# Retention in three bursts, its read-out turned by VectorE and DRAM, gate loads on SyncE

## The chip, the cores and the metric

The kernel runs on one core of a Trainium2 chip. The metric is the device time of one execution in microseconds (us), as the median of several runs; lower is better. Within the core TensorE (PE) multiplies matrices, VectorE (DVE), ScalarE (ACT) and GpSimd (POOL) work on tiles, and SyncE (SP) issues DMAs. ScalarE and GpSimd issue DMAs too, each in the order of its own instructions.

## The reference

Two layers of a decoder trunk on x of 512 x 1024, all float32. Each layer runs three branches of width 512 from one input projection, multiplies each by sigmoid gates after a branch projection, adds them, and goes on with an output projection and a gated MLP.

```python
for l in range(DEPTH):                       # 2 layers
    h = rmsnorm(x, norm1_g[l])
    p = h @ w_in[l]
    ...
    y_rw  = rwkv7_branch(p_rw, ...)          # branch 0
    y_ret = retention_branch(p_ret, cos, sin)  # branch 1
    y_sg  = sgu_branch(p_sg, ...)            # branch 2
    branches = jnp.stack([y_rw, y_ret, y_sg], axis=2)
    proj = jnp.einsum('bsgc,gcd->bsgd', branches, w_branch[l])
    gates = jax.nn.sigmoid(gate_logits.reshape(B, S, N_BRANCH, D_MODEL))
    x = x + jnp.sum(gates * proj, axis=2) @ w_out[l]
    x = x + conv_ffn(rmsnorm(x, norm2_g[l]), ...)
```

The retention branch, which the change rewrites, has 4 heads (q and k of 64, v of 128 columns) over 4 chunks of 128 positions; the scale and the gate at its end are applied per position and head:

```python
scores = jnp.einsum('bhnid,bhnjd->bhnij', qc, kc) * decay_in[:, None]
inner = jnp.einsum('bhnij,bhnje->bhnie', scores, vc)
kv = jnp.einsum('bhnjd,bhnje,hj->nbhde', kc, vc, k_dec)
...                                          # R_prev: running sum of kv with decay
cross = jnp.einsum('bhnid,nbhde,hi->bhnie', qc, R_prev, q_dec)
y = (inner + cross).transpose(0, 2, 3, 1, 4).reshape(B, S, RET_HEADS, RET_V_DIM)
y = y * lax.rsqrt(jnp.mean(y * y, axis=-1, keepdims=True) + EPS)
return (y.reshape(B, S, RET_V_WIDTH) * jax.nn.silu(g))
```

## The kernel before

Every large product is written as three matmuls of a high and a low part (lo x hi, hi x hi, hi x lo), each of 128 rows by 512 columns. A weight block of 128 x 512 goes through `unit`: SyncE loads it into one of three raw tiles (`wr`, line 123), ScalarE copies the high part (`sh` or `wh`, line 136), VectorE subtracts to get the low part (`sl` or `wl`, line 137), which frees the raw tile for the next load. The matmuls with both parts are line 153. `split` does the same to an activation (lines 145 and 146).

After the recurrence of branch 0, `mixer` runs through the steps of the string `SEQ` (both versions stand in the diff), in this order but for what the scheduler, which sets the order of the instructions on each engine, moves around. The steps are:

- `0`, `2` and `1`: a merge, `merge(l, br, m, ...)`: block m of the projection of branch 0, 2 or 1. It takes one weight unit, 12 matmuls into a PSUM tile `acc`, and VectorE multiplies that by the gate tile `gth` (line 1024), which comes back from DRAM (`gd`, line 1021), and adds it to the sum of the branches.
- `H`: `ret_heads` loads q and k of the retention branch, head by head, and copies parts of q (`qS`) and v (`vs`) to other partitions by DMAs on ScalarE's queue (line 882).
- `S`: one row of retention, `ret_row(read, score)`: the scores of chunk `score` (16 small matmuls), and for chunk `read` the products with scores and states (up to 32 small matmuls) into two PSUM tiles X; then ScalarE squares with a sum (`rss`, line 936), VectorE multiplies by the gate (line 938), GpSimd raises the sums to the power -1/2 (`rrr`, line 949), and ScalarE scales the four heads (line 952). `ret_states` adds 32 and 24 small matmuls (line 898) in the first two rows. There are five rows: score 0; read 0 and score 1; and so on to read 3.
- `G` and `U`: steps of branch 2 (`sgu_out`, 16 matmuls of 128 columns, line 1009; and a group of 24 matmuls of 512 columns).
- `Y`: `ret_out`: TensorE turns the 4 x 4 blocks of 128 x 128 of the scaled heads with 16 transposes (line 959) into PSUM, and `split` makes the high and low parts that the `1` merges read.

Of the kernel before, what the change touches and what calls it, by code (L numbers as in the profile page):

```python
# [17 lines left out]
S = 512  # L18
# [6 lines left out]
SEQ = "0 H 0 0 G G S U S U G S 0 G S 0 0 S 2 2 0 0 Y 2 2 1 2 1 2 1 2 1 2 1 1 1 1"  # L25
# [24 lines left out]
class Emit:  # L50
# [110 lines left out]
    def matF(self, ps, w, xs):  # L161
        for _ in self.matFg(ps, w, xs):
            pass

    def matFg(self, ps, w, xs):

        K = len(xs)
        for k0 in range(0, K, 4):
            nk = min(4, K - k0)
            hi, lo = self.unit(*w[:3], w[3] + k0 * 128, nk * 128)  # L170
            for j in range(nk):
                k = k0 + j
                sl = slice(j * 128, j * 128 + 128)
                self.mm3(ps, (hi[:, sl], lo[:, sl]), xs[k], k == 0, k == K - 1)
            yield
# [187 lines left out]
    def mixer(self, l, nst):  # L363
# [19 lines left out]
        rows = iter([(None, 0), (0, 1), (1, 2), (2, 3), (3, None)])  # L383
        for step in SEQ.split():
            if step == "S":
                self.ret_row(*next(rows))
            elif step == "G":
                ysg.append(self.sgu_out(len(ysg)))
            elif step == "H":
                self.ret_heads()  # L390
            elif step == "U":
                next(rest), next(rest)
            elif step == "Y":
                yret = self.ret_out()
            elif step == "0":
                mg.append(self.merge(l, 0, len(mg), yrw))
            elif step == "2":
                mg[m2] = self.merge(l, 2, m2, ysg, mg[m2])
                m2 += 1
            else:  # L400
                out.append(self.split(self.merge(l, 1, len(out), yret, mg[len(out)], self.nc.vector), self.f))
# [465 lines left out]
    def ret_heads(self):  # L867
# [3 lines left out]
        for j in range(4):  # L871
            t = self.r((128, 4, 128), n="qF" if j < 2 else "kF")
            self.nc.sync.dma_start(t.rearrange("p c t -> p (c t)"), self.qk[128 * j:128 * j + 128, :])
            (self.qF if j < 2 else self.kF).append(t)
# [31 lines left out]
    def ret_row(self, read, score):  # L906
# [5 lines left out]
        hd = [(j, p, h) for j in range(2) for p in range(2) for h in range(2)]  # L912
# [5 lines left out]
        if read is not None:  # L918
            v, g = self.vt[read], self.yg[read]
            for j, p, h in [(j, p, 1 - h) for j, p, h in hd]:  # L920
                i, o = 2 * j + h, h ^ j
                w = v[hv[p], 128 * i:128 * i + 128] if p == o else self.vs[read][hv[o], j, :]
                mm(o, p, X[o][hv[p], j, :], self.sc[hv[o], h, p, :], w, read == p == 0)
            for j, p, h in hd:
                if read or p:
                    o, ts = h ^ j, slice(128 * read + 64 * p, 128 * read + 64 * p + 64)
                    q = self.qS if j else self.qF[0].rearrange("p c t -> p (c t)")
                    mm(o, p, X[o][hv[p], j, :], q[hv[o], ts], self.Rs[2 * read + p][hv[o], j, :])
        if score is not None:
            for j, p, h in hd:  # L930
                ts = slice(64 * p, 64 * p + 64)
                mm(h, h ^ j, X[h][hv[h ^ j], 2, ts], self.kF[j][hv[h], score, ts], self.qF[j][hv[h], score, ts])
        if read is not None:
            sq, ss = self.u((128, 4, 128), n="rsq"), self.small((128, 4), "rss")
            for i in range(4):
                A.activation(sq[:, i, :], X[i % 2 ^ i // 2][:, i // 2, :], AF.Square, accum_out=ss[:, i:i + 1])
            for o in range(2):
                V.tensor_tensor(self.heads(g, o), X[o][:, 0:2, :], self.heads(g, o), op=MUL)
        if score is not None:
            sc = self.u((128, 2, 2, 64), n="sc")  # L940
            for h in range(2):
                V.tensor_tensor(sc[:, h], X[h][:, 2, :].rearrange("q (p t) -> q p t", t=64), self.c("le64").unsqueeze(1).to_broadcast([128, 2, 64]), op=MUL)
            self.sc = sc
            if score < 2:
                self.ret_states(4 * score, 4 + 3 * score)
        if read is not None:
            V.tensor_scalar(ss, ss, 4.0 / 128, 4e-6, op0=MUL, op1=ADD)
            rr = self.small((128, 4), "rrr")
            nc.gpsimd.tensor_tensor(rr, ss, self.c("mhalf")[:, 0:4], op=POW)
            for i in range(4):  # L950
                o = g[:, 128 * i:128 * i + 128]
                A.activation(o, o, AF.Copy, scale=rr[:, i:i + 1])

    def ret_out(self):
        out = []
        for h in range(4):
            pt = self.sm()
            for c in range(NC):
                self.tc.keep_in_program_order(self.nc.tensor.transpose(pt[:, c * 128:c * 128 + 128], self.yg[c][:, h * 128:h * 128 + 128], self.c("ident")))  # L959
            out.append(self.split(pt, self.f))  # L960
        return out
# [55 lines left out]
    def merge(self, l, br, m, y, sum=None, add=None):  # L1017

        nc = self.nc
        t = self.f(n="gth")  # L1020
        nc.gpsimd.dma_start(t, self.gd[br, m])
        ps = self.acc()
        self.matF(ps, ("wall", l, 58 + br * 4 + m // 2, m % 2 * 512), y)
# [277 lines left out]
```

## Time and profile before

| what | value |
|---|---|
| median of 3 runs | 1703.2 us (1702.57 to 1703.39) |
| profiled execution, whole | 1702.28 us |
| its span | 1700.6 us |
| granted TensorE clock, mean | 0.999 |
| busy: PE, DVE, ACT, POOL | 1692.3, 1141.6, 765.9, 245.4 us |

The span is the time between the first and the last instruction that the profiler saw in that one execution. Busy time of an engine is what its instructions took; where an engine is idle, the profile names the instruction that ended the wait. Layer 0 has its retention rows between 363 and 410 us, layer 1 between 1210 and 1255 us. In a timeline row stand start, duration, engine, line, operation, tiles, shape and count.

### The profile page before, as it was taken

Reading aid. Unit: us, or ns where it says so; the run is one execution under the profiler, and the core shown is the slowest. Engines: PE = TensorE matmul, PEld = TensorE weight load, DVE = VectorE, ACT = ScalarE, POOL = GpSimd, SP = SyncE. Lnnn points to the kernel's source line nnn. Section 1 sums busy time; section 2 is a strip of 40 time slices with the busy share of each in tenths; the row PEclk is TensorE's granted clock in tenths of the full one; section 3 lists DMA queues with packets and bytes.
Section 4 is the critical chain, followed back from the end, with each engine's and each line's share of the span. In section 5 each row is a group of like instructions: output and inputs, shape, how many; then the busy total and the mean of one; then the engine's idle time right before and its main releaser. Section 6 shows DMA issues by size and latency. Waiting matters only on the chain.

```text
span 1700.6 us, 28356 instructions
## 1 busy us (share of the span) xinstructions
PE 1692.3 (100%) x10564; PEld 1390.6 (82%) x10564; DVE 1141.6 (67%) x2032; ACT 765.9 (45%) x1341; POOL 245.4 (14%) x326
## 2 busy tenths in 40 slices
PE   9999999999999999999999999999999999999998
PEld 7888877888888888888888888778888888888887
DVE  7887856567569777653367786564765798876432
ACT  7564433535355444333255634345343554443322
POOL 1122235114100000000011203441141000000010
PEclk9999999999999999999999999999999999999999
DMA  5334566446443333243332346555364454432531
GB/s 175 91 101 151 147 151 152 141 130 194 137 149 100 96 97 99 69 119 110 115 113 80 112 142 155 148 141 161 108 210 141 132 138 123 124 107 68 155 100 55
DMA packets 151337, 214.20 MB, mean 126 GB/s; under 512 B 48416, under 2 KB 57248, under 8 KB 151200
## 3 DMA queue, kind: packets, MB, share of 16 engines
q1 hardware_dynamic: 129552, 171.62, 34.2%
q0 software_dynamic: 9600, 21.77, 4.9%
q10 hardware_dynamic: 12048, 19.00, 3.4%
q8 instruction: 83, 1.36, 0.3%
q14 instruction: 54, 0.44, 0.1%
HBM read 181.92 MB, written 23.07 MB: 121 GB/s over the span
## 4 chain that ended last, share of the span: by engine, by line
PE 99%; DMA 0%; ACT 0%; DVE 0%; issue 0%
PE acc L153 88%; PE sm L153 4%; PE sm L647 2%; PE acc L287 1%; PE sm L561 1%; PE sm L915 1%; PE acc L1009 0%; PE sm L524 0%; PE sm L523 0%; DMA g<-pcols 0%; PE sm L898 0%; PE sm L959 0%; PE sm L805 0%; PE sm L795 0%; PE sm L578 0%; PE sm L579 0%
## 5 line engine op out<-in xcount | busy, mean ns | idle before, releaser
L153 PE MATMUL acc<-lo,sh 128*128 128x512 f32 x1108 | 432.3, 390 | 0.0
L153 PE MATMUL acc<-hi,sh 128*128 128x512 f32 x1108 | 431.6, 390 | 0.0
L153 PE MATMUL acc<-hi,sl 128*128 128x512 f32 x1108 | 431.1, 389 | 0.0
L136 ACT CAST sh<-wr 128x512 fp32r<-128x512 f32 (+1 forms) x385 | 235.1, 615 | 380.2 <-PE acc L153 263.4
L137 DVE TENSOR_TENSOR sl<-wr,sh 128x512 fp32r<-128x512 f32 (+1 forms) x385 | 263.4, 687 | 170.5 <-ACT sh L136 104.8
L153 PEld LDWEIGHTS acc<-lo,sh 128*128 128x128 f32 x1108 | 208.0, 188 | 44.1 <-issue 0.7
L153 PEld LDWEIGHTS acc<-hi,sl 128*128 128x128 f32 x1108 | 208.0, 188 | 43.7 <-issue 0.3
L153 PEld LDWEIGHTS acc<-hi,sh 128*128 128x128 f32 x1108 | 208.0, 188 | 42.9 <-issue 0.2
L136 ACT CAST wh<-wr 128x512 fp32r<-128x512 f32 x194 | 120.2, 620 | 227.9 <-PE acc L153 209.2
L153 PE MATMUL acc<-lo,wh 128*128 128x512 f32 x556 | 219.4, 395 | 0.0
L153 PE MATMUL acc<-hi,wl 128*128 128x512 f32 x556 | 217.0, 390 | 0.0
L153 PE MATMUL acc<-hi,wh 128*128 128x512 f32 x556 | 216.6, 390 | 0.0
L137 DVE TENSOR_TENSOR wl<-wr,wh 128x512 fp32r<-128x512 f32 x195 | 138.9, 712 | 111.6 <-ACT wh L136 104.7
L153 PEld LDWEIGHTS acc<-hi,wl 128*128 128x128 f32 x556 | 104.4, 188 | 22.6 <-issue 0.7
L153 PEld LDWEIGHTS acc<-lo,wh 128*128 128x128 f32 x556 | 104.3, 188 | 22.6 <-issue 0.3
L153 PEld LDWEIGHTS acc<-hi,wh 128*128 128x128 f32 x556 | 104.4, 188 | 20.9
L153 PE MATMUL acc<-ah,sh 128*128 128x512 f32 x352 | 108.3, 389 | 0.0
L1077 DVE TENSOR_TENSOR fu<-acc,rsF 128x512 f32<-128x512 f32 x88 | 60.5, 689 | 62.3 <-PE acc L153 62.3
L1079 ACT ACTIVATE cv<-fu,pc 128x512 f32<-128x512 f32 x88 | 71.6, 816 | 50.4 <-DVE fu L1077 47.5
L153 PE MATMUL acc<-wl,hi 128*128 128x512 f32 x192 | 78.0, 406 | 0.0
L1080 DVE SCALAR_TENSOR_TENSOR cv<-fu,pc,cv 128x511 f32<-128x511 f32 x88 | 65.4, 746 | 18.6 <-ACT cv L1079 18.6
L153 PEld LDWEIGHTS acc<-ah,sh 128*128 128x128 f32 x352 | 66.1, 188 | 13.7
(335 smaller groups left out, 2450.1 us busy)
## 6 DMA issues: line engine op xcount, KB each, us to landing
wr<-wall SPq DMA_DIRECT2D x480, 256.0 KB, 2.7
gd<-gth ACTq DMA_DIRECT2D x48, 256.0 KB, 3.3
gth<-gd POOLq DMA_DIRECT2D x48, 256.0 KB, 3.3
wr<-wdt SPq DMA_DIRECT2D x44, 256.0 KB, 2.7
wr<-wdn SPq DMA_DIRECT2D x40, 256.0 KB, 2.7
x<-xT SPq DMA_DIRECT2D x8, 256.0 KB, 4.7
tn<-ysq POOLq DMA_DIRECT2D x32, 64.0 KB, 3.3
tab<-rot ACTq DMA_DIRECT2D x8, 256.0 KB, 3.9
```

Source lines behind the costliest of these rows:

```text
L136: self.kept((high or self.nc.scalar.copy)(hi[:, :n], raw[:, :n]))
L137: self.kept(self.nc.vector.tensor_tensor(lo[:, :n], raw[:, :n], hi[:, :n], op=SUB))
L153: i = self.nc.tensor.matmul(*x, **y, **kw)
L287: po(self.nc.tensor.matmul(pss[j], w[:, j * 128:j * 128 + 128], x, start=k == n == 0, stop=k == 7 and n == 2))
L561: i = T.matmul(pK[hv[1 - h], j, :], bk[hv[h], c, 1, :], x[hv[h], c, :], start=True, stop=True)
L647: po(T.matmul(o, l, r, start=start, stop=True, skip_group_check=True))
L915: po(T.matmul(o, lhsT, rhs, start=new[b][q], stop=stop, skip_group_check=True))
L1077: V.tensor_tensor(u, ps, self.rsF, op=MUL)
L1079: A.activation(t, u, AF.Identity, scale=self.p("cw2", j), bias=self.p("cb", j))
L1080: V.scalar_tensor_tensor(t[:, 1:], u[:, :511], self.p("cw1", j), t[:, 1:], op0=MUL, op1=ADD)
```

## The change

Retention is cut into three bursts instead of five rows: the first computes the scores of all four chunks and the first states, the second reads chunks 0 and 1 and adds the other states, the third reads chunks 2 and 3. The read-out leaves TensorE: VectorE turns 32 x 32 blocks of the scaled heads into four tiles `yz`; 16 DMAs on ScalarE's queue (64 KB each, 512 bytes a piece) write them to a DRAM tile; four SyncE loads bring it back as `yF` in the order of columns that the merges need; ScalarE and VectorE make the two parts. In `SEQ` ten merges now stand between the last `S` and the first `1`. The gate loads of the merges move from GpSimd's queue to SyncE's, in program order behind the weight's load of the same merge; those of branches 1 and 2 take their tiles from another pool. `ret_heads` loads its four tiles in another order.

```diff
@@ -22,7 +22,7 @@
 RWC, RETC, SGC = 1792, 1536, 1024
 NU, NR, NFP = 31, 16, 39
 FILL = (35, 2, 1)
-SEQ = "0 H 0 0 G G S U S U G S 0 G S 0 0 S 2 2 0 0 Y 2 2 1 2 1 2 1 2 1 2 1 1 1 1"
+SEQ = "0 H 0 0 0 G G S U U G S 0 G S 0 0 2 2 0 2 2 2 2 Y 2 1 2 1 1 1 1 1 1 1"
 NRAW = 3
 START = "z0 w0 z1 w1 z2 w2 z3 s0 z4 s1 w3 z5 s2 s3 w4 z6 s4 w5 z7 s5 s6 w6 s7 w7"
 AHEAD = {None: 2, "p": 4, "r": 3, "f": 3, "u": 5}
@@ -158,16 +158,18 @@
         mm(ps, wh, xh, start=False, stop=False)
         mm(ps, wl, xh, start=False, stop=stop)
 
-    def matF(self, ps, w, xs):
-        for _ in self.matFg(ps, w, xs):
+    def matF(self, ps, w, xs, then=None):
+        for _ in self.matFg(ps, w, xs, then):
             pass
 
-    def matFg(self, ps, w, xs):
+    def matFg(self, ps, w, xs, then=None):
 
         K = len(xs)
         for k0 in range(0, K, 4):
             nk = min(4, K - k0)
             hi, lo = self.unit(*w[:3], w[3] + k0 * 128, nk * 128)
+            if then:
+                then()
             for j in range(nk):
                 k = k0 + j
                 sl = slice(j * 128, j * 128 + 128)
@@ -380,10 +382,10 @@
         yrw, ysg, mg, out, m2 = self.yrw, [], [], [], 0
         self.pool = "r"
         rest = self.sgu_u(l, range(2, 4))
-        rows = iter([(None, 0), (0, 1), (1, 2), (2, 3), (3, None)])
+        rows = iter([None, 0, 2])
         for step in SEQ.split():
             if step == "S":
-                self.ret_row(*next(rows))
+                self.ret_row(next(rows))
             elif step == "G":
                 ysg.append(self.sgu_out(len(ysg)))
             elif step == "H":
@@ -868,7 +870,7 @@
 
         A, V, T, po = self.nc.scalar, self.nc.vector, self.nc.tensor, self.tc.keep_in_program_order
         self.qF, self.kF = [], []
-        for j in range(4):
+        for j in (0, 2, 1, 3):
             t = self.r((128, 4, 128), n="qF" if j < 2 else "kF")
             self.nc.sync.dma_start(t.rearrange("p c t -> p (c t)"), self.qk[128 * j:128 * j + 128, :])
             (self.qF if j < 2 else self.kF).append(t)
@@ -903,61 +905,75 @@
             else:
                 V.tensor_tensor(self.Rs[n + 1], self.Rs[n], at(n), op=ADD)
 
-    def ret_row(self, read, score):
+    def ret_row(self, read):
 
 
         nc, V, A, T, po = self.nc, self.nc.vector, self.nc.scalar, self.nc.tensor, self.tc.keep_in_program_order
         hv = [slice(0, 64), slice(64, 128)]
         X, new = [self.sm((128, 4, 128)) for _ in range(2)], [[True, True], [True, True]]
-        hd = [(j, p, h) for j in range(2) for p in range(2) for h in range(2)]
+        hd = [(j, p, h) for j in range(2) for p in range(2) for h in (1, 0)]
 
         def mm(b, q, o, lhsT, rhs, stop=True):
             po(T.matmul(o, lhsT, rhs, start=new[b][q], stop=stop, skip_group_check=True))
             new[b][q] = False
 
-        if read is not None:
-            v, g = self.vt[read], self.yg[read]
-            for j, p, h in [(j, p, 1 - h) for j, p, h in hd]:
+        if read is None:
+            for c in range(NC):
+                for j, p, h in hd:
+                    ts = slice(64 * p, 64 * p + 64)
+                    mm(h, h ^ j, X[h][hv[h ^ j], c, ts], self.kF[j][hv[h], c, ts], self.qF[j][hv[h], c, ts])
+            self.ret_states(0, 4)
+            self.sc = [self.u((128, 8, 64), n="sc") for _ in range(2)]
+            for h in range(2):
+                V.tensor_tensor(self.sc[h], X[h].rearrange("q c (p t) -> q (c p) t", t=64), self.c("le64").unsqueeze(1).to_broadcast([128, 8, 64]), op=MUL)
+            return
+        cs = range(read, read + 2)
+        for c in cs:
+            for j, p, h in hd:
                 i, o = 2 * j + h, h ^ j
-                w = v[hv[p], 128 * i:128 * i + 128] if p == o else self.vs[read][hv[o], j, :]
-                mm(o, p, X[o][hv[p], j, :], self.sc[hv[o], h, p, :], w, read == p == 0)
+                w = self.vt[c][hv[p], 128 * i:128 * i + 128] if p == o else self.vs[c][hv[o], j, :]
+                mm(o, p, X[o][hv[p], 2 * (c - read) + j, :], self.sc[h][hv[o], 2 * c + p, :], w, c == p == 0)
+        for c in cs:
             for j, p, h in hd:
-                if read or p:
-                    o, ts = h ^ j, slice(128 * read + 64 * p, 128 * read + 64 * p + 64)
+                if c or p:
+                    o, ts = h ^ j, slice(128 * c + 64 * p, 128 * c + 64 * p + 64)
                     q = self.qS if j else self.qF[0].rearrange("p c t -> p (c t)")
-                    mm(o, p, X[o][hv[p], j, :], q[hv[o], ts], self.Rs[2 * read + p][hv[o], j, :])
-        if score is not None:
-            for j, p, h in hd:
-                ts = slice(64 * p, 64 * p + 64)
-                mm(h, h ^ j, X[h][hv[h ^ j], 2, ts], self.kF[j][hv[h], score, ts], self.qF[j][hv[h], score, ts])
-        if read is not None:
-            sq, ss = self.u((128, 4, 128), n="rsq"), self.small((128, 4), "rss")
+                    mm(o, p, X[o][hv[p], 2 * (c - read) + j, :], q[hv[o], ts], self.Rs[2 * c + p][hv[o], j, :])
+        if read == 0:
+            self.ret_states(4, 7)
+        ss = self.small((128, 2, 4), "rss")
+        for c in cs:
+            sq, g = self.u((128, 4, 128), n="rsq"), self.yg[c]
             for i in range(4):
-                A.activation(sq[:, i, :], X[i % 2 ^ i // 2][:, i // 2, :], AF.Square, accum_out=ss[:, i:i + 1])
+                A.activation(sq[:, i, :], X[i % 2 ^ i // 2][:, 2 * (c - read) + i // 2, :], AF.Square, accum_out=ss[:, c - read, i:i + 1])
             for o in range(2):
-                V.tensor_tensor(self.heads(g, o), X[o][:, 0:2, :], self.heads(g, o), op=MUL)
-        if score is not None:
-            sc = self.u((128, 2, 2, 64), n="sc")
-            for h in range(2):
-                V.tensor_tensor(sc[:, h], X[h][:, 2, :].rearrange("q (p t) -> q p t", t=64), self.c("le64").unsqueeze(1).to_broadcast([128, 2, 64]), op=MUL)
-            self.sc = sc
-            if score < 2:
-                self.ret_states(4 * score, 4 + 3 * score)
-        if read is not None:
-            V.tensor_scalar(ss, ss, 4.0 / 128, 4e-6, op0=MUL, op1=ADD)
-            rr = self.small((128, 4), "rrr")
-            nc.gpsimd.tensor_tensor(rr, ss, self.c("mhalf")[:, 0:4], op=POW)
+                V.tensor_tensor(self.heads(g, o), X[o][:, 2 * (c - read):2 * (c - read) + 2, :], self.heads(g, o), op=MUL)
+        V.tensor_scalar(ss, ss, 4.0 / 128, 4e-6, op0=MUL, op1=ADD)
+        rr = self.small((128, 2, 4), "rrr")
+        nc.gpsimd.tensor_tensor(rr, ss, self.c("mhalf")[:, 0:8].rearrange("p (c i) -> p c i", i=4), op=POW)
+        if read == 0:
+            self.yd, self.yz = self.turned(), [self.u((128, 4, 4, 32), n="yz") for _ in range(4)]
+        for c in cs:
             for i in range(4):
-                o = g[:, 128 * i:128 * i + 128]
-                A.activation(o, o, AF.Copy, scale=rr[:, i:i + 1])
+                o = self.yg[c][:, 128 * i:128 * i + 128]
+                A.activation(o, o, AF.Copy, scale=rr[:, c - read, i:i + 1])
+                V.transpose(self.yz[i][:, :, c, :], o.rearrange("p (b f) -> p b f", f=32))
+        for i in range(4) if read else ():
+            d = self.yd[128 * i:128 * i + 128].rearrange("(b f) (q t) -> f b q t", b=4, q=4)
+            for q in range(4):
+                nc.scalar.dma_start(d[:, :, q, :], self.yz[i][32 * q:32 * q + 32].rearrange("f b c t -> f b (c t)"))
 
     def ret_out(self):
+
         out = []
-        for h in range(4):
-            pt = self.sm()
-            for c in range(NC):
-                self.tc.keep_in_program_order(self.nc.tensor.transpose(pt[:, c * 128:c * 128 + 128], self.yg[c][:, h * 128:h * 128 + 128], self.c("ident")))
-            out.append(self.split(pt, self.f))
+        for i in range(4):
+            t = self.u(n="yF")
+            self.tc.keep_in_program_order(self.nc.sync.dma_start(t, self.yd[128 * i:128 * i + 128, :]))
+            t = t.rearrange("p (q c t) -> p c q t", q=4, c=4)
+            hi, lo = [self.f((128, 4, 4, 32), F32R, n) for n in ("hi", "lo")]
+            self.nc.scalar.copy(hi, t)
+            self.nc.vector.tensor_tensor(lo, t, hi, op=SUB)
+            out.append([o.rearrange("p c q t -> p (c q t)") for o in (hi, lo)])
         return out
 
 
@@ -1017,10 +1033,9 @@
     def merge(self, l, br, m, y, sum=None, add=None):
 
         nc = self.nc
-        t = self.f(n="gth")
-        nc.gpsimd.dma_start(t, self.gd[br, m])
+        t = (self.u if br else self.f)(n="gth")
         ps = self.acc()
-        self.matF(ps, ("wall", l, 58 + br * 4 + m // 2, m % 2 * 512), y)
+        self.matF(ps, ("wall", l, 58 + br * 4 + m // 2, m % 2 * 512), y, lambda: self.tc.keep_in_program_order(nc.sync.dma_start(t, self.gd[br, m])))
         nc.vector.scalar_tensor_tensor(t, t, 1.0, ps, op0=ADD, op1=MUL)
         if sum is None:
             return t
```

Three places show how the instructions stand. First ScalarE in layer 0, from the scales of the last chunks on (`vt` are the scaled heads, `sh` high parts of weights, `tn` the DRAM tile, `hi<-sm` and `hi<-yF` the high parts of the turned heads). Before:

```order
L136 CAST sh_4758<-wr_4675 128x512
L136 CAST sh_4781<-wr_4733 128x512
L952 ACTIVATE vt_3747<-vt_3747,rrr_4598 128x128 x4
L136 CAST sh_4808<-wr_4756 128x512
L136 CAST sh_4831<-wr_4779 128x512
L145 CAST hi_4699<-sm_4694 128x512
```

And after:

```order
L959 ACTIVATE vt_3742<-vt_3742,rrr_4565 128x128 x4
L959 ACTIVATE vt_3747<-vt_3747,rrr_4565 128x128 x4
L136 CAST sh_4738<-wr_4691 128x512
L964 DMA tn_4460<-yz_4461 32x4x128 x4
L964 DMA tn_4460<-yz_4462 32x4x128 x4
L964 DMA tn_4460<-yz_4463 32x4x128 x4
L964 DMA tn_4460<-yz_4464 32x4x128 x4
L136 CAST sh_4761<-wr_4713 128x512
L136 CAST sh_4784<-wr_4736 128x512
```

Two chunks are scaled together, and 16 DMA issues stand between two weight casts; the casts of `yF` come six weight casts later.

Second, SyncE's queue in the same stretch. Before, it holds little but weights' loads:

```order
L123 DMA wr_4675<-wall 128x512
L123 DMA wr_4733<-wall 128x512
L1036 DMA xi_5086<-xT 128x512
L123 DMA wr_4756<-wall 128x512
L123 DMA wr_4779<-wall 128x512
```

After, gate loads and the loads of `yF` stand among them:

```order
L123 DMA wr_4782<-wall 128x512
L1038 DMA gth_4780<-gd_2547 128x512
L123 DMA wr_4829<-wall 128x512
L123 DMA wr_4852<-wall 128x512
L971 DMA yF_4803<-tn_4460 128x512
L971 DMA yF_4809<-tn_4460 128x512
L971 DMA yF_4815<-tn_4460 128x512
L123 DMA wr_4879<-wall 128x512
L971 DMA yF_4821<-tn_4460 128x512
```

The first three `yF` loads stand behind the load of the weight `wr_4852`, and every load that waits for its tile holds those behind it.

Third, TensorE around step `Y`. Before, the transposes stand between two merges:

```order
L153 MATMUL acc_4674<-hi_4102,sl_4610 128x512
L959 MATMUL sm_4694<-con,vt_3732 128x128
L959 MATMUL sm_4694<-con,vt_3737 128x128
L959 MATMUL sm_4694<-con,vt_3742 128x128
L959 MATMUL sm_4694<-con,vt_3747 128x128
L959 MATMUL sm_4703<-con,vt_3732 128x128
```

After, the first merge of branch 1 (`acc_4851`) follows the tenth merge behind the last burst (`acc_4828`), and a merge of branch 2 (`acc_4878`) stands between its first and its later matmuls:

```order
L153 MATMUL acc_4828<-hi_4511,sl_4739 128x512
L153 MATMUL acc_4851<-lo_4806,sh_4761 128x512
L153 MATMUL acc_4851<-hi_4805,sh_4761 128x512
L153 MATMUL acc_4851<-hi_4805,sl_4762 128x512
L153 MATMUL acc_4878<-lo_4228,sh_4784 128x512
L153 MATMUL acc_4878<-hi_4227,sh_4784 128x512
L153 MATMUL acc_4878<-hi_4227,sl_4785 128x512
L153 MATMUL acc_4878<-lo_4240,sh_4784 128x512
```

TensorE's transposes are gone, and its first need of a turned head is `lo_4806`, the low part of `yF_4803`.

## The prediction

> **What bounds the kernel now.** I read the page first, then the waits of TensorE, then its timeline around the retention rows of layer 0.
>
> ```profile
> span 1700.6 us, 28356 instructions
> PE 1692.3 (100%) x10564; PEld 1390.6 (82%) x10564; DVE 1141.6 (67%) x2032; ACT 765.9 (45%) x1341; POOL 245.4 (14%) x326
> PEclk9999999999999999999999999999999999999999
> PE 99%; DMA 0%; ACT 0%; DVE 0%; issue 0%
> PE acc L308 <- DVE rst L305: 1.5, 1, 1.5
> PE acc L287 <- DVE wh L136: 0.4, 1, 0.4
> ```
>
> TensorE is busy for the whole span, the chain that ended last is 99% TensorE, and the last two rows are all that its list of waits holds: 1.9 us, at the start. So a change gains only what it takes off TensorE's stream, and any wait that it puts there is paid in full. The profiled execution took 1702.28 us (1700.6 of span and 1.7 around it), 0.9 below the median of 1703.2; I work out differences and add them to both. A measurement of this kernel tells about 0.2%, 3.4 us, from no change.
>
> **What TensorE saves.** The next rows are TensorE's timeline: start, duration, line, output and inputs.
>
> ```profile
> 369.56 0.39 PE L153 MATMUL acc<-hi,sl 128*128 128x512 f32 x1
> 369.88 0.47 PE L915 MATMUL sm<-qF,kF 64*64 64x64 f32 x16
> 370.16 1.07 PE L898 MATMUL sm<-vt,ro 64*64 64x128 f32 x32
> 371.16 0.50 PE L153 MATMUL acc<-lo,sh 128*128 128x512 f32 x1
> 371.50 0.40 PE L153 MATMUL acc<-hi,sh 128*128 128x512 f32 x1
> ...
> 386.88 0.39 PE L153 MATMUL acc<-hi,sl 128*128 128x512 f32 x1
> 387.11 1.05 PE L1009 MATMUL acc<-ws,sgv 128*128 128x128 f32 x8
> 387.92 0.48 PE L153 MATMUL acc<-lo,sh 128*128 128x512 f32 x1
> 388.23 0.40 PE L153 MATMUL acc<-hi,sh 128*128 128x512 f32 x1
> ...
> 397.27 0.39 PE L153 MATMUL acc<-hi,sh 128*128 128x512 f32 x1
> 397.59 0.32 PE L915 MATMUL sm<-vs,sc 64*64 64x128 f32 x1
> 398.62 0.50 PE L153 MATMUL acc<-hi,sl 128*128 128x512 f32 x1
> 398.96 0.40 PE L153 MATMUL acc<-lo,sh 128*128 128x512 f32 x1
> ...
> 405.14 0.39 PE L153 MATMUL acc<-lo,sh 128*128 128x512 f32 x1
> ...
> 406.96 0.39 PE L153 MATMUL acc<-hi,sl 128*128 128x512 f32 x1
> 407.19 1.91 PE L959 MATMUL sm<-con,vt 128*128 128x128 f32 x16
> 408.85 0.48 PE L153 MATMUL acc<-lo,sh 128*128 128x512 f32 x1
> 409.17 0.39 PE L153 MATMUL acc<-hi,sh 128*128 128x512 f32 x1
> ```
>
> From 405.14 to 406.96 are eight matmuls of 512 columns: 0.2275 us each, so a merge of 12 takes 2.73. The 16 transposes of step Y stand between 406.96 and 409.17: 2.21 less two steps of 0.2275 is 1.75 us. They go. A burst of small matmuls also pays at its borders: at 369.56 the next start comes 0.32 later, 0.09 over a step, and after it the starts at 371.16 and 371.50 are 0.34 apart, 0.11 over: 0.20 per burst. Five bursts S become three, so two borders go, 0.41 us. Scores, states and reads stay as many as before. Per layer 1.75 + 0.41 = 2.16 us; the second layer has the same order, so 4.3 us in all, if nothing waits.
>
> **What is put in its place.** The way from the scaled heads to TensorE was 16 transposes; now it is 16 VectorE transposes, 16 DMAs on ScalarE's queue, 4 loads of 256 KB on SP's, a cast and a subtraction for each. TensorE has ten merges between the last burst and the first "1" merge (acc_4851 in layer 0), whose first matmul reads lo_4806. Durations for the chain, by line (min/median/max in ns) or timeline:
>
> ```profile
> 385.18 0.27 ACT L936 ACTIVATE rsq<-sm 128x128 f32<-128x128 f32 x1
> 386.98 0.16 DVE L947 TENSOR_SCALAR rss<-rss 128x4 f32<-128x4 f32 x1
> 388.71 1.28 ACT L952 ACTIVATE vt<-vt,rrr 128x128 f32<-128x128 f32 x4 [0.78 <-POOL rrr L949]
> 389.90 1.12 ACT L136 CAST sh<-wr 128x512 fp32r<-128x512 f32 x2
> L949 POOL TENSOR_TENSOR rrr<-rss,con x8: 1027/1200/1388, 378.8 to 1249.0; 128x4 f32<-128x4 f32 x8
> L1051 DVE STREAM_TRANSPOSE xz<-xi x32: 266/271/311, 1359.4 to 1503.0; 128x128 f32<-128x128 f32 x32
> L1054 SPq DMA_DIRECT2D xr<-xz x32: 325/426/478, 1360.4 to 1505.2; - x32
> L423 ACTq DMA_DIRECT2D gd<-gth x48: 326/332/362, 101.4 to 1086.3; - x48
> L882 ACTq DMA_DIRECT2D vs<-vt x16: 607/620/1732, 359.2 to 1209.9; - x16
> L727 SPq DMA_DIRECT2D yF<-tn x8: 326/424/428, 336.9 to 1185.7; - x8
> DMA to landing us min/median/max: 2.8/4.1/4.9
> L137 DVE TENSOR_TENSOR sl<-wr,sh x385: 418/686/1817, 46.0 to 1664.3; 128x512 fp32r<-128x512 f32 x185, 128x256 fp32r<-128x256 f32 x8
> wr<-wall SPq DMA_DIRECT2D x480, 256.0 KB, 2.7
> ```
>
> *When TensorE needs it.* Let t = 0 be the end of the reads of the second burst. Then come 24 state matmuls (32 take 370.16 to 371.16, so 0.75) and a border (0.11), a merge (2.73), the G step (386.88 to 388.23 less two steps: 0.90), the third burst (64 reads; 32 take 397.59 to 398.62, so 2.06 and 0.20 of borders: 2.27) and ten merges (27.3): **+34.1**.
>
> *When it is ready.* Chunks 0 and 1 first. Their squares and head products: one chunk took 1.8 us from its first square to rss (385.18 to 386.98); for two I take 3.0, between eight squares of 0.27 in a row (2.2) and twice 1.8 (3.6). From rss to the first scale were 1.73 with a power of 1.39; with the median 1.20 it is 1.54: +4.5. Eight scales at 0.30 (388.71 to 389.90 for four): +6.9; their transposes (0.27 each) follow on VectorE and end 0.3 later. Then ScalarE casts a weight tile and VectorE subtracts (0.6 and 0.69), which frees a raw tile: +8.2; its load lands 2.7 later, +10.9; three casts (0.55 each, by 389.90) stand ahead of the squares of chunks 2 and 3 in ScalarE's order: +12.6, though their PSUM was ready at +6.8. Again 3.0, 1.54 and 2.4: +19.5. One cast: +20.1. Now the 16 issues. No DMA of this shape stands on ScalarE's queue; L1054 has the shape (32x4x128, 64 KB) on SP's, at 0.426; L423, a plain 128x512, costs 0.332 on ScalarE, L882 (a copy inside SBUF) 0.62. I take 0.43, as the shape is the same: 6.9 us, **+27.0**. These issues go ahead of the weight casts in ScalarE's order. Behind them a cast and three subtractions (0.62 + 0.69 + 2 x 0.62) free three raw tiles: +29.5. SP has to issue those weights first, since the first yF load stands behind wr_4852 (0.33 for its issue): +29.9. yF lands 4.1 later, +34.0; cast and subtraction 1.3: **+35.3**.
>
> So it is late by **1.2 us**. The last link has no cover at all; the yF of the later heads arrive under matmuls of a "2" merge that stand between. Ends for the unknown prices: issues at 0.33 take 1.6 off, at 0.62 add 3.1; landing 2.8 or 4.9 is -1.3 or +0.8; squares at 2.2 or 3.6 twice -1.6 or +1.2 (the power's 1.03 and 1.39 are +-0.3). With the lower ends it isn't late and the stall is 0; with the upper ones it is 4 to 6 us.
>
> **The other edits.** Sixteen VectorE transposes add 16 x 0.27 = 4.3 us per layer on an engine that is 67% busy, and ScalarE (45%) gets 6.9 us of issues; neither bounds. Both are counted where they stand in the chain.
>
> ```profile
> SPq L123 <- DVE sl L137: 772.2, 362, 18.9
> L1021 POOL DMA_DIRECT2D gth<-gd x48: 536/538/734, 354.6 to 1286.9; - x48
> gth<-gd POOLq DMA_DIRECT2D x48, 256.0 KB, 3.3
> ```
>
> The 24 gate loads per layer go from GpSimd (0.54 each) to SP, behind the weights' load of their merge. SP waits 772 us for raw tiles, so 0.33 each costs it nothing; GpSimd's power isn't late for it any more. What it may cost is order: a gate now lands 3.3 us behind an issue that waits for the raw tile, and until it has landed, VectorE can't empty the merge's PSUM bank. By the same chain the gate of the fifth merge after the last burst has 0.4 us to spare: cost 0, and if that cover goes, a wait of that size moves ahead of the one above and takes its place rather than adds, since the chain of yF doesn't wait for it. The order of the loads of qF and kF and of h in the reads has no price: the same instructions in another order, with the burst still behind them by a merge.
>
> **The sum.** Per layer -2.16 + 1.2 = -0.96; twice, -1.9. Profiled 1702.28 becomes 1700.4, the median 1703.2 becomes **1701.3**.
>
> [...]
>
> **Rivals.**
> *A, no stall.* The detour ends in time. It needs a lateness under 0.45 us per layer (where the gain still passes 3.4 us), so only 0.75 us less than my sum; L423's price does it alone (-1.6). Against it: all 16 issues are in a row on one queue, and four waits follow one another with nothing between. Time 1703.2 - 4.3 = **1698.9**. [...]
> *B, the issues on ScalarE's queue are the price.* At L882's 0.62 the chain is late by 1.2 + 3.1 = 4.3 us per layer: -2.16 + 4.3 = +2.1, twice +4.3: **1707.5**, slower. It decides from a lateness of 3.9 us per layer (2.16 + 1.7). For it: L882 is the only copy on that queue out of an SBUF tile with broken rows. Against it: L423 there is at 0.33, like SP's plain loads, so the queue by itself isn't dearer.
> *C, the clock.* The page's clock row, quoted first, is at nine tenths or more in every slice, with TensorE never idle, so no row here tells what an idle stretch does. If a stall of some 3 us dropped the clock to half, the matmuls behind it would take 0.455 instead of 0.2275 for a while; ten of them are 2.3 us per layer, so B becomes some 1712. [...]
>
> **Chances.** Forecast (a stall of 0.45 to 3.85 us per layer, its own range 1699.8 to 1706.6): 0.42. A: 0.40. B with C: 0.18. So faster 0.40, same 0.42, slower 0.18. The range runs from A less 0.6 for the borders (0.1 each way in a burst) to the upper end of the forecast, 1698.3 to 1706.6; B lies outside.
>
> **What would show it.** TensorE's list of waits should have two new rows at L153 for lo of yF (L975), about 1.2 us each. L959 as TensorE's transposes gone, and some 4.3 us less between the other bursts. ScalarE's 16 DMAs at L964 in one row, 6 to 8 us long; SP's L971 behind them by about 3 us. Right for A: no wait on TensorE beyond 1.9 us. Wrong for all: waits on TensorE at the gates' or at the weights' lines (L1042 or L137), or bursts that cost over 0.2 us more than their parts.

## The result and the profile after

The changed kernel takes 1713.8 us (1712.64 to 1714.45, 4 runs) against 1702.94 for the kernel before: a ratio of 1.0063, 95% interval 1.005 to 1.0076. The forecast was 1701.3 with a range up to 1706.6, so it is slower where "no change" was forecast. The page of the changed kernel, and the rows of TensorE's list of waits that are new:

```profile
span 1711.5 us, 28332 instructions
PE 1692.0 (99%) x10532; PEld 1389.4 (81%) x10532; DVE 1150.0 (67%) x2048; ACT 768.1 (45%) x1341; POOL 217.5 (13%) x274
PE 95%; DMA 2%; DVE 1%; ACT 1%; issue 0%; POOL 0%; ACTq 0%; SPq 0%; DVEq 0%; POOLq 0%
PE acc L153 <- DVE lo L975: 10.3, 2, 5.4
PE acc L153 <- DVE lo L146: 0.6, 2, 0.4
PE acc L153 <- DVE gth L1039: 0.3, 1, 0.3
```

The first of them is the one that the prediction named: two waits for the low part of the first turned head (L975), one in each layer. They are 4.9 and 5.4 us, not 1.2. The chain that ended last now leaves TensorE, for the links of the detour. TensorE's timeline around the wait in layer 0:

```profile
420.67 0.39 PE L153 MATMUL acc<-hi,sl 128*128 128x512 f32 x1
425.96 0.79 PE L153 MATMUL acc<-lo,sh 128*128 128x512 f32 x1 [4.90 <-DVE lo L975]
426.55 0.63 PE L153 MATMUL acc<-hi,sh 128*128 128x512 f32 x1
...
428.69 0.63 PE L153 MATMUL acc<-lo,sh 128*128 128x512 f32 x1
429.11 0.43 PE L153 MATMUL acc<-hi,sh 128*128 128x512 f32 x1
```

From 420.67 to 425.96 are 5.29 us, 5.06 over a step. Then come matmuls at a step of 0.43 instead of 0.2275 (426.55 to 428.69 is five steps, 2.14) until 429.11. The granted clock has dropped from 1.00 to 0.50, as the profile's busy times of two stretches show (stretch, its length, busy time and count of PE, PE's weight loads, DVE, ACT and POOL, then the granted TensorE clock, the DMA share and GB/s):

```profile
422.37:425.78 3.41, 0.00 (x0) 0.00 (x0) 2.40 (x4) 2.41 (x4) 1.26 (x1) 1.00 0.99 334
425.78:429.20 3.42, 3.24 (x8) 2.56 (x9) 3.42 (x5) 1.92 (x4) 1.66 (x1) 0.50 1.00 359
```

In layer 0 the seven slow steps cost 1.56 us, in layer 1, where the granted clock is 0.50 from 1272.29 to 1279.12, eight cost 1.76.

The 10.9 us by which the span grew add up from TensorE's starts in both layers: the small matmuls -5.2 (their bursts take 10.87 us of a layer over the plain steps, 13.49 before), the two waits +10.6 (5.06 and 5.54), the slow steps +3.3, four short waits ahead (0.3 to 0.6 each) +1.7, elsewhere +0.3: together +10.7.

The links of the detour in layer 0, from the timelines of ScalarE, GpSimd, VectorE and SyncE:

```profile
386.31 0.62 ACT L145 CAST hi<-sgm 128x512 fp32r<-128x512 f32 x1 [1.35 <-DVE sgm L1029]
386.84 0.27 ACT L948 ACTIVATE rsq<-sm 128x128 f32<-128x128 f32 x1
390.03 1.64 POOL L953 TENSOR_TENSOR rrr<-rss,con 128x8 f32<-128x8 f32 x1 [29.19 <-DVE rss L951]
391.71 2.45 ACT L959 ACTIVATE vt<-vt,rrr 128x128 f32<-128x128 f32 x8 [2.36 <-POOL rrr L953]
400.67 0.27 ACT L948 ACTIVATE rsq<-sm 128x128 f32<-128x128 f32 x1
405.55 2.45 ACT L959 ACTIVATE vt<-vt,rrr 128x128 f32<-128x128 f32 x8 [1.85 <-POOL rrr L953]
407.70 0.34 ACTq L964 DMA_DIRECT2D tn<-yz  x1
408.08 8.36 ACTq L964 DMA_DIRECT2D tn<-yz  x15
416.49 1.66 ACT L136 CAST sh<-wr 128x512 fp32r<-128x512 f32 x3 [7.97 <-DMA tn<-yz]
417.86 0.33 SPq L123 DMA_DIRECT2D wr<-wall  x1
418.29 0.82 SPq L1038 DMA_DIRECT2D gth<-gd  x1
419.20 0.86 SPq L123 DMA_DIRECT2D wr<-wall  x2
420.23 1.29 SPq L971 DMA_DIRECT2D yF<-tn  x3
424.56 1.94 ACT L974 CAST hi<-yF 128x512 fp32r<-128x512 f32 x3 [0.36 <-DMA yF<-tn]
425.21 1.35 DVE L975 TENSOR_TENSOR lo<-yF,hi 128x512 fp32r<-128x512 f32 x2
```

With t = 0 at 385.7, the end of the second burst's reads, they stand against the prediction like this:

| link ends | predicted | measured |
|---|---|---|
| first scale of chunks 0, 1 | +4.5 | +6.0 (391.71) |
| squares of chunks 2, 3 begin | +12.6 | +15.0 (400.67) |
| their scales are done | +19.5 | +22.3 |
| the 16 issues are done | +27.0 | +30.7 (416.44) |
| the first yF load is issued | +29.9 | +34.5 (420.23) |
| its cast begins | +34.0 | +38.9 (424.56) |
| TensorE has lo | +35.3 | +40.3 (425.96) |
| TensorE needs lo | +34.1 | +35.2 |
| late | 1.2 | 5.1 |

### The profile page after: what moved, and what is told of

The parts are those of the page before. It is cut to its first block, busy times and chain, and to the rows that moved or that the text cites. A ratio compares the mean times of both kernels' runs of the same rounds, so it can differ in the third digit from the quotient of the medians.

```text
span 1711.5 us, 28332 instructions
## 1 busy us (share of the span) xinstructions
PE 1692.0 (99%) x10532; PEld 1389.4 (81%) x10532; DVE 1150.0 (67%) x2048; ACT 768.1 (45%) x1341; POOL 217.5 (13%) x274
## 4 chain that ended last, share of the span: by engine, by line
PE 95%; DMA 2%; DVE 1%; ACT 1%; issue 0%; POOL 0%; ACTq 0%; SPq 0%; DVEq 0%; POOLq 0%
PE acc L153 85%; PE sm L153 4%; PE sm L649 2%; PE acc L289 1%; DMA wr<-wall 1%; PE sm L563 1%; ACT rsq L948 0%; ACT sh L136 0%; POOL rrr L953 0%; DVE sl L137 0%; DMA yF<-tn 0%; DMA x<-xT 0%; DVE yz L960 0%; DMA tn<-yz 0%; PE sm L526 0%
## 5 line engine op out<-in xcount | busy, mean ns | idle before, releaser
L153 PE MATMUL acc<-lo,sh 128*128 128x512 f32 x1108 | 433.2, 392 | 11.3 <-DVE lo L975 10.3
```

The source lines that it names most:

```text
L153: i = self.nc.tensor.matmul(*x, **y, **kw)
```

## The experiments

All are the changed kernel with one edit, unless said otherwise. The kernel before, on the same chip, took 1702.55 us beside the transposes on TensorE, twelve merges, four writes and the gates back on GpSimd; 1702.93 beside thirteen merges, the gates alone, the split queues and the writes on GpSimd; 1703.12 beside eleven merges, the double writes and thirteen merges with gates on GpSimd; 1702.78 beside the last three. A ratio is against that time, with its 95% interval.

**Where the loss is: without the detour, and with more cover.** The first run puts the 16 transposes back on TensorE and leaves the writes and reads out:

```diff
-                V.transpose(self.yz[i][:, :, c, :], o.rearrange(...))
...
+                self.tc.keep_in_program_order(self.nc.tensor.transpose(pt[:, c * 128:c * 128 + 128], ...))
```

> The changed kernel, but TensorE turns the heads again as before (16 transposes per layer, no DRAM detour). Theory A (the loss is the wait for the first turned head, 4.9 and 5.4 us, and the 7 to 8 matmuls at the slower clock behind each, some 1.6 us): both vanish, TensorE keeps only the saving of the merged bursts. By the changed kernel's rows the bursts hold 10.87 us of a layer, with 1.75 for the transposes 12.62 against 13.49 before, so 0.87 per layer less; the short waits at lo L146 and the gate's line (up to 0.8 us per layer) may stay: 1701.2 to 1702.8. Theory B (the gates behind the weights on SyncE's queue hold up the merges): the waits stay wherever the heads are turned, over 1705.

Measured: 1701.47 us (ratio 0.9992, 0.9983 to 1.0001). All waits on yF and all slow matmuls are gone. Theory B falls: the gates stand behind the weights here too.

Merges moved behind the last burst:

```diff
-SEQ = "0 H 0 0 0 G G S U U G S 0 G S 0 0 2 2 0 2 2 2 2 Y 2 1 2 1 ..."
+SEQ = "0 H 0 0 0 G G S U U G S 0 G S 0 0 2 2 0 2 2 2 2 Y 2 2 1 1 ..."    # eleven
+SEQ = "0 H 0 0 G G S U U G S 0 G S 0 0 0 2 2 0 2 2 2 2 Y 2 2 1 1 ..."    # twelve
+SEQ = "0 H 0 0 G G S U U G S G S 0 0 0 0 2 2 0 2 2 2 2 Y 2 2 1 1 ..."    # thirteen
```

> The changed kernel, but with twelve merges instead of ten between the last burst and the first merge of branch 1 (a merge of branch 0 and one of branch 2 moved there). Theory A: TensorE needs the first head 2 x 2.73 = 5.46 us later, as much as the wait was; no wait or one under 0.5 us and no slow matmuls: 1713.8 - 10.3 - 3.3 = about 1700.2. Theory B: the merges moved carry their gate loads along, the wait stays at 2 us or more per layer: over 1705.

> The changed kernel, but with thirteen merges between the last burst and the first merge of branch 1 (five of branch 0 and all eight of branch 2 there). Theory A (what the change costs is the wait for the first turned head and the slow matmuls behind it): with twelve a wait of 1.2 us per layer was left, one merge more is 2.73, so no wait on yF at all: the time with twelve, 1701.3, less 2.4 = 1698.9. Theory B (moving merges only moves the wait, since weights and gates of the moved merges are late elsewhere): waits turn up ahead of the bursts and the time stays at 1701 or more.

> The changed kernel, but with eleven merges between the last burst and the first merge of branch 1: the one behind the tenth, of branch 2, goes ahead of it, and nothing ahead of the last burst moves. Theory A (the chain has its own length, TensorE waits for the rest, and a long wait slows the clock): the wait falls by one merge, 2.73, to 2.2 and 2.7 us per layer, and the 7 to 8 slow matmuls behind it are gone: 1713.8 - 2 x 2.73 - 3.3 = 1705.0. Without a price of the clock: 1708.3. Theory D (the chain is held by what TensorE frees, so it grows with each merge put in front): the wait stays near 5 us, 1712 or more.

Measured: eleven 1708.59, twelve 1701.27, thirteen 1699.81 us (ratio 0.9983, 0.9974 to 0.9992). TensorE's waits on yF, in that order:

```profile
PE acc L153 <- DVE lo L975: 5.9, 4, 2.8
PE acc L153 <- DVE lo L975: 2.4, 2, 1.3
PE acc L153 <- DVE lo L975: 0.3, 1, 0.3
```

With ten it was 10.3. The eleventh merge takes 4.4 of that, most of 2 x 2.73, as it should if the chain has its own length; theory D falls. With twelve the first head is in time in both layers (in layer 0 its low part is ready at 422.76 and read at 423.26). The 2.4 us left are waits for the last head's, whose subtraction VectorE does behind a weight's of 1.8 us. Thirteen is the only version that beats both kernels clearly: 3.1 us below the kernel before, 4.3 being what the prediction gave for no stall. Against the three bursts with TensorE's transposes (1701.47) it gains 1.7 us, but the two intervals overlap, and those transposes were not run with thirteen merges.

With eleven the clock still drops, which was not expected. TensorE's timeline with eleven, and in the run with four writes (below), around a wait of almost the same length:

```profile
423.77 0.39 PE L153 MATMUL acc<-hi,sl 128*128 128x512 f32 x1
426.71 0.67 PE L153 MATMUL acc<-lo,sh 128*128 128x512 f32 x1 [2.55 <-DVE lo L975]
427.19 0.63 PE L153 MATMUL acc<-hi,sh 128*128 128x512 f32 x1
427.61 0.63 PE L153 MATMUL acc<-hi,sl 128*128 128x512 f32 x1
```

```profile
420.07 0.39 PE L153 MATMUL acc<-hi,sl 128*128 128x512 f32 x1
423.38 0.47 PE L153 MATMUL acc<-lo,sh 128*128 128x512 f32 x1 [2.91 <-DVE gth L1039]
423.68 0.40 PE L153 MATMUL acc<-hi,sh 128*128 128x512 f32 x1
423.92 0.40 PE L153 MATMUL acc<-hi,sl 128*128 128x512 f32 x1
```

A gap of 2.94 from start to start is followed by slow steps (0.42), one of 3.31 by steps of 0.24 (423.68 to 423.92). So 1708.6 is the expectation's other sum, 1708.3, in which the price of the clock isn't taken off. Two stretches around the gap with eleven, then two with four writes:

```profile
423.46:426.87 3.41, 0.86 (x5) 0.40 (x4) 2.29 (x4) 2.69 (x5) 0.64 (x1) 1.00 1.04 385
426.87:430.29 3.42, 3.42 (x9) 2.54 (x9) 3.42 (x5) 1.60 (x3) 1.66 (x1) 0.50 1.00 353
418.72:422.14 3.42, 1.74 (x8) 1.12 (x6) 1.50 (x3) 1.99 (x4) 0.00 (x0) 1.00 0.50 124
422.14:425.55 3.41, 1.63 (x6) 1.05 (x6) 3.41 (x5) 1.32 (x3) 1.68 (x1) 1.00 0.55 170
```

With eleven the granted clock is 0.50 from 426.87 to 430.29; with four writes it is 1.00 in both stretches, though the gap is longer. So the length of the gap doesn't tell these two runs apart, and what does is not shown. That a wait of 1 to 3 us is too short to slow the clock, as the expectation with the gates back on GpSimd has it (below), was an estimate: with eleven the steps behind a wait of 2.55 us are slow.

**The gates.** Alone, in the kernel before (merge, matF and matFg as in the change):

> The kernel before, with one part of the change alone: the gate loads of the merges on SyncE's queue behind the weight's load, with their tiles as in the change. Theory A: SyncE and VectorE have slack there, no wait on TensorE: the time of the kernel before within 0.5 us (1702 to 1703). Theory B (late gates hold PSUM banks): waits on TensorE at the gate's line, 1704 or more.

Measured: 1703.26 us (1.0001, 0.9992 to 1.0010), no wait at the gate's line. And back on GpSimd, in the changed kernel and with thirteen merges:

```diff
-        self.matF(ps, ("wall", ...), y, lambda: ...(nc.sync.dma_start(t, self.gd[br, m])))
+        nc.gpsimd.dma_start(t, self.gd[br, m])
+        self.matF(ps, ("wall", ...), y)
```

> The changed kernel, but the gate loads go from GpSimd again, issued ahead of the weight's load. Theory A: the 16 issues on ScalarE stay, the reads of the heads stand behind fewer loads on SyncE and the casts of yF directly behind the issues: the first head comes some 2 to 4 us earlier, a wait of 1 to 3 us per layer is left, too short to slow the clock: 1702 to 1706. Theory B: all waits go, 1699.

> Thirteen merges between the last burst and the first merge of branch 1, and the gate loads on GpSimd again. Theory A (where the gates go costs nothing of its own): 1699 to 1701, as with thirteen merges and gates on SyncE. Theory E (eleven gate issues on GpSimd stand ahead of the power for chunks 2 and 3, each behind a free tile, and hold the chain): waits on TensorE come back, at the low part of a branch 2 activation or of yF, over 1704.

Measured: 1714.11 and 1702.86 us (the second 0.9998, 0.9988 to 1.0007). Neither theory held for the first: TensorE waited 8.2 us for the low parts of branch 2 (L146) and 3.2 for yF, and in layer 0 a weight cast ahead of such a cast waited 6.8 us for its load. That load was cast 5.6 us after its issue at 396.32, in the changed kernel 2.7; ahead of it GpSimd had issued ten gate loads in a row (391.03 to 396.63), and the DMA engines were full from 394 to 400 (share 0.96 and 1.02, in the changed kernel 0.15 and 0.68). That points at the gate loads, but no run separates it. With thirteen merges the time also lies between the two theories, 3 us above the same order with gates on SyncE, though the two intervals overlap; 2.8 us of waits on yF came back.

**Which link of the detour.** Four large writes, the sorting moved to the reads:

```diff
-            for q in range(4):
-                nc.scalar.dma_start(d[:, :, q, :], self.yz[i][32 * q:32 * q + 32]...)
+            nc.scalar.dma_start(self.yd[128 * i:128 * i + 128, :], self.yz[i]...)
...
+            for b in range(4):
+                ...(self.nc.sync.dma_start(t[32 * b:32 * b + 32]..., d[:, :, b, :]))
```

> The changed kernel, but the DRAM tile holds the turned blocks as they lie in yz: 4 writes of 256 KB on ScalarE's queue for each layer instead of 16 of 64 KB; the sorting moves to SyncE's reads, four of 64 KB for each head. Theory A: the 16 issues in a row took 8.7 us of ScalarE, four at 0.33 take 1.3; three more reads ahead of the first head cost 3 x 0.43 = 1.3 us. The first head is ready some 6 us earlier, more than it was late, so neither wait nor slow matmuls: about 1700. Theory B: the gates' queue is unchanged, so 1710 or more.

Every second write on SyncE's queue (`(nc.scalar, nc.sync)[q % 2]`), or all on GpSimd's (`nc.gpsimd`):

> The changed kernel, but every second of the 16 writes goes on SyncE's queue instead of ScalarE's. Theory A (the row of 16 issues on ScalarE is the longest link): ScalarE is free 8 x 0.49 = 3.9 us earlier and the one wait for a finished transfer inside the row (1.0 us) may go; the wait on yF falls from 5.1 to 0 to 1.2 us and the slow matmuls vanish: 1700 to 1703. Theory C (what holds the chain is SyncE's order: weights ahead of yF, each behind a raw tile and a finished transfer): SyncE has eight more issues ahead of the weights, the wait stays at 4 us or more: 1711 or more.

> The changed kernel, but the 16 writes are issued by GpSimd. Theory A: ScalarE casts weights without the 8.7 us break, SyncE's loads follow, and the first head needs only its own four writes (4 x 0.54 = 2.2 us of issue): it comes some 5 us earlier, no wait or under 1 us, no slow matmuls: 1699 to 1702. Theory C: SyncE's order holds the chain as before, wait of 4 us or more: 1711 or more.

Measured: 1716.01, 1711.13 and 1712.30 us; all three missed what theory A expected. They are the times of theories B and C, but without C's wait of 4 us on yF in each layer. The lists of waits say why:

```profile
PE acc L153 <- DVE gth L1039: 5.7, 2, 2.9
PE acc L153 <- DVE lo L975: 4.6, 4, 2.5
```

```profile
PE acc L153 <- DVE lo L975: 6.3, 4, 1.9
```

```profile
PE acc L153 <- DVE gth L1039: 4.8, 3, 3.9
PE acc L153 <- ACT sh L136: 3.1, 1, 3.1
PE acc L153 <- DVE lo L975: 2.5, 3, 2.1
```

The waits on yF fell in all three, by 4 to 8 us (with four writes the first low part was ready at 420.73 instead of 425.90), so the row of writes is on the path. But others came: with four writes the 16 reads hold the gates behind them on SyncE; split, the weights stand behind the writes there, and each layer waits twice, 1.6 us on average; on GpSimd the cast of yF waits in ScalarE's order and holds the weight casts behind it. So the row of writes isn't the only long link.

Each write issued twice, the second into a tile that nothing reads:

> The changed kernel, but ScalarE issues every one of the 16 writes a second time, into a second DRAM tile that nothing reads, behind the first 16. Theory A (the row of issues is on the path to the first head): 16 more at a step of 0.49 and one or two waits of 1 us inside the row make the wait longer by 8 to 9.5 us in each layer, to 13 to 15 us: 1730 to 1733. Theory C (SyncE's loads and the landing are the path, ScalarE has slack): the wait grows by under 3 us, 1714 to 1720.

Measured: 1723.02 us in one run, between the two theories. The wait in layer 0 is 14.0 us, 9.1 longer, which is the second row itself; in layer 1 it is 6.6, only 1.2 longer, though the second row is 9.0 long there too. The difference is the order that the scheduler chose: in layer 1 the four yF loads went ahead of the weights on SyncE and the casts directly behind the writes.

```profile
1264.10 9.29 ACTq L964 DMA_DIRECT2D tn<-yz  x15
1273.60 9.02 ACTq L970 DMA_DIRECT2D tn<-yz  x16
1282.72 0.62 ACT L136 CAST sh<-wr 128x512 fp32r<-128x512 f32 x1 [18.28 <-DMA tn<-yz]
1283.24 0.61 ACT L980 CAST hi<-yF 128x512 fp32r<-128x512 f32 x1
1268.63 6.52 SPq L977 DMA_DIRECT2D yF<-tn  x4
```

That order was then tried by itself, with the change's ten merges, with eleven, and (third) only by a scheduler's priority on the loads. In the string, `Y` moves ahead of two merges (the expectation says four):

```diff
-... G S 0 0 2 2 0 2 2 2 2 Y 2 1 2 1 1 ..."
+... G S 0 0 2 2 0 2 2 Y 2 2 2 1 2 1 1 ..."    # ten
+... G S 0 0 2 2 0 2 2 Y 2 2 2 2 1 1 1 ..."    # eleven
...
+            with self.tc.high_priority():
                 self.tc.keep_in_program_order(self.nc.sync.dma_start(t, self.yd[...]))
```

> The changed kernel with its ten merges, but step Y stands four merges earlier in the string: SyncE then issues the four loads of the turned heads ahead of the next weights' loads, and ScalarE casts the first head directly behind the 16 writes. No instruction is added or taken away. Theory F (the links behind the writes, six weight casts and three weights' loads ahead of the first head's cast, are what makes it late): the first head is loaded under the row of writes and is ready some 2 us after its end, 6 to 7 us earlier than with the change, so no wait on it and no slow matmuls; weights and gates behind it may cost up to 1 us: 1700 to 1702. Theory A alone (the writes themselves are too late): the wait stays at 3 us or more, 1707 or more.

> As the run with the loads first, and with eleven merges ahead of the first merge of branch 1. Theory F: the head is 3 us early already, so the eleventh adds nothing: the same time within 0.5 us, and 1699 if a small wait was left. Theory A alone: the wait falls by 2.7 us against ten merges.

> The changed kernel, but the loads of the turned heads have a higher priority in the scheduler: on SyncE each goes ahead of one or two weights' loads, and the first head's cast stands behind four weight casts instead of six. Theory F: half of the links behind the writes go, so the wait falls by 1 to 2.5 us to some 3 to 4 us per layer, with the slow matmuls in part: 1706 to 1710. Theory A alone: no change, 1713 to 1714.

Measured: 1704.67 (1.0010, 1.0001 to 1.0019), 1705.53 and 1710.14 us. With the loads first, the same 16 writes and the same ten merges:

```profile
408.80 8.53 ACTq L964 DMA_DIRECT2D tn<-yz  x15
417.37 0.62 ACT L974 CAST hi<-yF 128x512 fp32r<-128x512 f32 x1 [8.14 <-DMA tn<-yz]
411.76 8.50 SPq L971 DMA_DIRECT2D yF<-tn  x4
PE acc L153 <- DVE gth L1039: 3.5, 5, 1.2
PE acc L153 <- DVE lo L975: 0.5, 2, 0.2
```

The first load goes out at 411.76, under the row of writes; the cast follows the last write. The wait on yF is 0.5 us in all, no matmul is slow, and 9.1 us of the change's loss are gone. From the last read of the second burst to the low part the chain takes 33 and 32 us in the two layers, not 40 and 41. The time is still 2.7 us above theory F's upper end, and above the kernel before: SyncE stands 8.5 us in its four loads, and the gates behind them come late (L1039, 3.5 us). The eleventh merge takes the last wait on yF away and gains nothing: 0.9 us more, where F allowed 0.5, but the intervals overlap (1.0014, 1.0005 to 1.0023), with 4.9 us of waits on gates. With the priority the first load in layer 0 goes out hardly earlier (420.16, not 420.23), but its cast begins at 422.96 instead of 424.56; 6.4 us of waits and slow steps in both layers were left, as F said, and the time is at the upper end of its range.

## Why the prediction was wrong

**What bounds, and the saving: right, the saving too small.** TensorE was the bound, and each wait on it was paid in full. Taken off were 2.6 us per layer, not 2.16: the bursts also joined the G steps, so more borders went than the two that I counted.

**The place of the stall: right.** One new wait per layer, on L975, in the first "1" merge.

**The size of the stall: the step that failed.** The chain measured 40.3 against 35.3, so the sum "when it is ready" came out 5.0 us short. No one term did it. Link by link, as in the table, it was short by 1.5 up to the first scale, 0.9 up to the next squares, 0.4 up to their scales, 0.9 over the issues, 0.9 up to the first yF load, and 0.4 for its landing, cast and subtraction. The first scale came 1.5 later (a cast of branch 2 stood ahead of the squares, and a power on 8 columns took 1.64, not the median of 4 columns, 1.20; it counts twice). Ahead of the next squares stood another cast of branch 2 and a wait of 0.62 for a weight. The row of 16 issues took 8.7 us at 0.55 each, against 6.9 at 0.43: the median of an issue was right at 0.444, but the issues of the row also had gaps between them, and in each layer one was long (1.05 and 0.80 us). Half of the row's excess was made good, as its first issue and the weight cast that the sum put ahead of the row ran beside one another and the last scale.

```profile
L964 ACTq DMA_DIRECT2D tn<-yz x32: 309/444/527, 407.7 to 1264.8; - x32
```

From the last issue to the first yF load it was 3.8 instead of 2.9 (a gate's issue of 0.82 stands between the weights), the landing 4.3. TensorE's need came 1.1 later than reckoned. The sum took middle values for links that follow one another, and the errors all had one sign. The prediction's own upper ends gave 4 to 6 us, which holds what was measured, but its range stopped at 3.85. Rival B had the right outcome for a part of the reason: it put the whole excess on the price of one issue (0.62), and the stretch of the issues was 0.9 us of the 5.0. B with C, at some 1712, came nearest to 1713.8; part of that is luck, as its stall was too short and its clock too dear.

**The clock: undervalued.** Rival C was held to be far off, as the stall was 1.2 us. At 4.9 and 5.4 us it cost 3.3, where C had 2.3 in each layer. C's stall of some 3 us with ten matmuls at 0.455 behind it was an estimate that no run shows: the changed kernel had seven and eight slow steps of 0.43 behind its waits of 4.90 and 5.38 us. Of the shorter gaps, one of 2.94 us (eleven merges) had eight slow steps behind it and one of 3.31 (four writes) none, so these runs give no length from which the clock drops.

**No cost for the gates on SyncE: right in this place, wrong where the order changes.** Alone they cost nothing (1703.26). But the change puts weights, gates and yF loads on one queue, and in the run with the loads first the gates became the next wait.

**What held the cover was the order behind the writes.** The prediction took it as given and priced it. The runs show it as the lever: with the loads ahead of the next weights the same detour fits under ten merges, but for 0.5 us of waits.

## What to carry to other kernels

A detour off the bounding engine is worth its saving only if its whole chain fits under the work in between, with margin: here 5.2 us were taken off and the shortfall cost 10.6 plus 3.3 for the clock. Add the issues of a row of DMAs with their gaps, not their median, take serial chains at the upper ends of their links, and look at what the scheduler put on each queue ahead of the last link. For a late chain, more cover (three merges) or an earlier place in the queue (four loads) took the wait on it away here (0.3 and 0.5 us were left), though the second left 1704.7 us, as other loads then came late. Moving the issues to another engine only moved the wait here.

## What the runs showed of the hardware

- DMAs issued in a row on ScalarE: 0.444 us median for one, 0.55 per issue over 16. The four of 256 KB in the other layout took 2.2 us, 0.54 each, so here four times the size cost no more for each.
- A power on 8 columns took 1.64 us on GpSimd, on 4 columns 1.20.
- TensorE's granted clock in the changed kernel was 0.50 from 425.78 to 429.20 us and from 1272.29 to 1279.12, at waits of 4.90 and 5.38 us; the steps of the matmuls were 0.43 there, where 0.2275 is the step at 1.00. A gap of 2.94 us in one run (eleven merges) had eight slow steps behind it; behind gaps of 3.31 and 3.48 us in two others (four writes, the writes on GpSimd) the steps were 0.23 to 0.24 from the second on.
